# The diagonal products of a chunked SSD, issued in two halves of 64 stationary columns

## The chip, the core and the metric

The kernel runs on one NeuronCore of one Trainium2 chip. TensorE multiplies: a load instruction puts the stationary operand (up to 128 x 128) into its array, and a product instruction streams the moving operand (up to 512 columns) through it into PSUM. VectorE, ScalarE and GpSimd work elementwise; 16 DMA engines move data. The metric is the device time of one execution in microseconds (us), as the median of the runs on record. Matrix products are done in one of two number forms: plain fp32, or F32R, a rounded fp32 for which the kernel splits each operand into a high and a low part and sums three products (the helper `mm3`, lines 403 to 406).

## The reference, cut to what matters

One layer of an encoder over 512 tokens of width 1024: layer norm, a mixer of neighbourhood attention and a bidirectional Mamba-2 SSD, and a squared-ReLU MLP. The SSD has 8 groups of 4 heads of width 64, state 128, and works in 4 chunks of 128 tokens. The part that the change touches is the product within a chunk, `y_diag`:

```
seg = a_cs[..., :, None] - a_cs[..., None, :]
lmat = jnp.exp(jnp.where(tril, seg, -jnp.inf))
cb = jnp.einsum('bclgn,bcsgn->bcgls', cc, bc)
y_diag = jnp.einsum('bcgls,bcgrls,bcsgrp->bclgrp', cb, lmat, xc)
...
y = y_f + y_b + xs * d_skip
```

For each group, chunk and head that is a 128 x 128 matrix of decays times scores, applied to 128 x 64 values. The kernel joins both directions in one such matrix.

## The kernel before, in words

Five stages follow each other on TensorE: the first layer norm and its transposes, the projections with the SSD (L977 last at 470.7 us), attention, the merge of the branches with the output projection, and the MLP. In the first two, the work is a list of steps (`op(engine, us, function, reads, writes)`). A planner (`Plan`, from line 109) ranks them by the longest way to the end, with the hand-given price of each step, and orders each engine's steps; the order at the beginning is written out by hand (`HEAD`, line 72). Steps marked `filler` are the large projections: they fill TensorE whenever no SSD step is ready.

For each of the 8 groups, `ssd` (from line 849) does on TensorE: transposes of B and x to tokens (L858, L878), the scores `cb` = B C for each chunk (L868), the chunk states `st` (L929, L941), the diagonal products `yd` (L977), and the products with the states, `yo` (L991). The matrix for `yd` is made in the tile `bc`: a DMA brings the running sums of the decays, VectorE and GpSimd subtract (L963), VectorE joins the directions (L967), ScalarE takes the exponential (L969), VectorE multiplies by the scores (L971).

`f_yd` (lines 975 to 979) then issues, for one chunk, four products, one a head: stationary is `bc()[:, 1, h, :]`, 128 x 128, moving is `xtok`, 128 x 64. The results of four heads lie beside each other in 256 columns of the tile `yd`, a PSUM bank that holds two chunks. The pool of banks has one for `yd` (`BANKS`, line 41). Both operands are plain fp32; each call shows in the trace as two loads and two products. `f_yd` is one step of the plan with a price of 0.9 us, and is called 32 times. VectorE adds `yd` to the off-diagonal part (L1011), and GpSimd multiplies the sum by the gate (L1021); transposed and split, it is the moving operand of the projection `ps_sbr`.

Three other places of TensorE's work matter below. `ps_dt` (helper lines 404 to 406) uses F32R tiles of 64 stationary columns (`wh_dt`, `wl_dt`, L584 and L585), and writes partitions 0 to 63. `ps_acsT` (L739) has plain fp32 operands, 32 stationary columns, and writes partitions 0 to 31. `tp_dt` (L681) transposes tiles of 64 rows.

## Time and profile before

| | |
|---|---|
| median of 3 runs | 1184.75 us (1184.36 to 1185.21) |
| profiled execution | span 1182.6 us |
| TensorE, products | 1159.1 us busy, 6138 instructions |
| TensorE, loads of weights | 990.3 us busy, 6138 instructions |
| VectorE, ScalarE, GpSimd | 757.7, 614.7, 545.2 us busy |
| DMA | 149.19 MB, 126 GB/s |
| L977, products | 256, in 31.0 us, 270 ns each |
| L977, loads | 256, in 31.5 us, 191 ns each |

PE are TensorE's products, PEld its loads, which run beneath the products. A form such as `128*64 128x256` means 128 rows and 64 columns of the array in use, and a moving operand of 128 x 256. The start of a product in the trace is when the array's queue takes it: a product that has to wait for its weights is shown longer than one that does not. Ends of products are modelled.

### The profile page before, as it was taken

The numbers are of one execution on the slowest core, as the hardware profiler recorded it, in microseconds if no ns is written. First come the engines' busy times: TensorE is split into PE (matmuls) and PEld (weight loads), VectorE is DVE, ScalarE is ACT, GpSimd is POOL, SyncE is SP. The second block draws the span as 40 slices with busy tenths as digits, with TensorE's granted clock in tenths as the row PEclk, the third lists the DMA queues.
The fourth block names the chain that finished last, engine by engine and source line by source line (L and its number), as shares of the span: only waits on it lengthen the run. The fifth ranks groups of instructions, "written<-read, shape, count | busy, mean of one in ns | idle before, by whom it ended". The sixth has DMA issues, their size and how long they took to land.

```text
span 1182.6 us, 16453 instructions
## 1 busy us (share of the span) xinstructions
PE 1159.1 (98%) x6138; PEld 990.3 (84%) x6138; DVE 757.7 (64%) x1363; ACT 614.7 (52%) x1033; POOL 545.2 (46%) x588
## 2 busy tenths in 40 slices
PE   5999999999999999999999999999999999999997
PEld 5988798989888888888888888888988888878886
DVE  7757475666656656443789975556543658488856
ACT  6676573837354654423667864342253545365410
POOL 1268968777788786304567540016046121222000
PEclk9999999999999999999999999999999999999999
DMA  6353333333333331333333223544236977889511
GB/s 201 97 157 125 102 130 107 112 116 129 102 114 107 126 120 59 107 105 85 87 87 86 56 71 107 166 147 138 85 107 184 237 187 200 192 211 233 160 51 54
DMA packets 129407, 149.19 MB, mean 126 GB/s; under 512 B 22960, under 2 KB 101808, under 8 KB 129328
## 3 DMA queue, kind: packets, MB, share of 16 engines
q1 hardware_dynamic: 115696, 112.63, 31.0%
q0 software_dynamic: 13056, 34.61, 11.9%
q8 instruction: 48, 0.79, 0.3%
q10 hardware_dynamic: 576, 0.92, 0.2%
q14 instruction: 31, 0.25, 0.1%
HBM read 145.90 MB, written 2.23 MB: 125 GB/s over the span
## 4 chain that ended last, share of the span: by engine, by line
PE 86%; DMA 4%; DVE 4%; issue 2%; POOL 2%; ACT 1%; SPq 1%; DVEq 0%; POOLq 0%; ACTq 0%
PE ps_f L406 8%; PE ps_f L404 8%; PE ps_f L405 8%; PE ps_x L406 5%; PE ps_x L404 5%; PE ps_x L405 4%; PE ps_abr L1368 4%; PE ps_z L404 3%; PE ps_z L405 3%; PE ps_z L406 3%; PE ps_sbr L404 2%; PE ps_sbr L406 2%; PE ps_sbr L405 2%; PE yd L977 2%; DMA w2r<-in_w_ff 2%; PE ps_g L405 2%
## 5 line engine op out<-in xcount | busy, mean ns | idle before, releaser
L784 DVE SCALAR_TENSOR_TENSOR cv<-ps_x,pc,cv 128x511 f32<-128x511 f32 (+1 forms) x128 | 95.7, 748 | 25.6 <-ACT cv L776 22.0
L405 PE MATMUL ps_f<-h1Th,wl_f 128*128 128x512 f32 (+1 forms) x288 | 104.0, 365 | 0.0
L404 PE MATMUL ps_f<-h1Th,wh_f 128*128 128x512 f32 (+1 forms) x288 | 103.6, 365 | 0.0
L406 PE MATMUL ps_f<-h1Tl,wh_f 128*128 128x512 f32 (+1 forms) x288 | 102.0, 365 | 0.0
L1571 DVE TENSOR_TENSOR wl_f<-w2r,wh_f 128x1024 fp32r<-128x1024 f32 x42 | 50.0, 1220 | 62.5 <-ACT wh_f L1570 62.2
L404 PE MATMUL ps_z<-wh_z,hTh 128*128 128x256 f32 x256 | 75.2, 294 | 0.6 <-DVE cv L784 0.5
L406 PE MATMUL ps_z<-wl_z,hTh 128*128 128x256 f32 x256 | 71.5, 279 | 0.0
L405 PE MATMUL ps_z<-wh_z,hTl 128*128 128x256 f32 x256 | 71.5, 279 | 0.0
L1565 POOL DMA_DIRECT2D w2r<-in_w_ff x30 | 36.3, 1415 | 75.6 <-DMA w2r<-in_w_ff 49.0
L405 PE MATMUL ps_f<-wh_f,sql 128*128 128x512 f32 x168 | 65.3, 390 | 0.5 <-DVE sql L1571 0.5
L406 PE MATMUL ps_f<-wl_f,sqh 128*128 128x512 f32 x168 | 65.3, 390 | 0.1
L1570 ACT ACTIVATE wh_f<-w2r 128x1024 fp32r<-128x1024 f32 x42 | 42.6, 1052 | 43.1 <-DMA w2r<-in_w_ff 32.8
L404 PE MATMUL ps_f<-wh_f,sqh 128*128 128x512 f32 x168 | 64.9, 389 | 0.0
L1099 DVE TENSOR_TENSOR ysacc<-ps_sbr,ysacc 128x512 f32<-128x512 f32 x56 | 38.6, 690 | 39.9 <-PE ps_sbr L406 39.7
L404 PEld LDWEIGHTS ps_f<-h1Th,wh_f 128*128 128x128 f32 x288 | 53.9, 188 | 9.0 <-ACT rl L1672 0.2
L405 PEld LDWEIGHTS ps_f<-h1Th,wl_f 128*128 128x128 f32 x288 | 53.9, 188 | 8.7
L387 DVE TENSOR_TENSOR wl_f<-ws_f,wh_f 128x1024 fp32r<-128x1024 f32 x36 | 47.2, 1347 | 20.9 <-ACT wh_f L386 20.7
L406 PEld LDWEIGHTS ps_f<-h1Tl,wh_f 128*128 128x128 f32 x288 | 52.8, 188 | 8.7
L404 PE MATMUL ps_x<-hTh,wh_bc 128*128 128x512 f32 (+1 forms) x144 | 56.7, 394 | 0.0
L404 PE MATMUL ps_sbr<-yTh,wh_sbr 128*128 128x512 f32 x128 | 55.6, 434 | 0.7 <-ACT yTh L1076 0.4
L406 PE MATMUL ps_x<-hTl,wh_bc 128*128 128x512 f32 (+1 forms) x144 | 53.4, 371 | 1.7 <-DVE hTl L626 1.7
L404 PE MATMUL ps_x<-hTh,wh_x 128*128 128x512 f32 (+1 forms) x144 | 54.6, 379 | 0.0
(344 smaller groups left out, 3734.2 us busy)
## 6 DMA issues: line engine op xcount, KB each, us to landing
ws_f<-in_w_ff SPq DMA_DIRECT2D x20, 1024.0 KB
w2r<-in_w_ff POOLq DMA_DIRECT2D x18, 1024.0 KB, 7.6
bc<-acs_d SPq DMA_DIRECT2D x32, 512.0 KB
w2r<-in_w_ff POOLq DMA_DIRECT2D x30, 512.0 KB, 8.8
ws_bc<-in_w_in SPq DMA_DIRECT2D x16, 512.0 KB
ws_x<-in_w_in SPq DMA_DIRECT2D x8, 1024.0 KB
ws_z<-in_w_in SPq DMA_DIRECT2D x8, 1024.0 KB
ws_g<-in_w_in SPq DMA_DIRECT2D x8, 1024.0 KB
```

Source lines behind the costliest of these rows:

```text
L387: (eng[i] if isinstance(eng, tuple) else eng).tensor_tensor(out=lo[:, k], in0=st[:, k], in1=hi[:, k].bitcast(F32), op=ALU.subtract)
L404: nc.tensor.matmul(o, lh, rh, start=start, stop=False)
L405: nc.tensor.matmul(o, ll, rh, start=False, stop=False)
L406: return nc.tensor.matmul(o, lh, rl, start=False, stop=stop)
L784: op("DVE", 0.75, lambda j=j, o=o, n=n: nc.vector.scalar_tensor_tensor(out=acc()[:, o], in0=ps()[:, n], scalar=tap(j), in1=acc()[:, o], op ...
L977: nc.tensor.matmul(yd()[:, c % 2, h * HD : (h + 1) * HD], bc()[:, 1, h, :], xtok()[:, c, h * HD : (h + 1) * HD], start=True, stop=True)
L1099: op("DVE", 0.69, lambda d=d, ps=ps: nc.vector.tensor_tensor(out=ysacc[:, d, :], in0=ps(), in1=ysacc[:, d, :], op=ALU.add), r=[(ps.name, 0 ...
L1368: ins.append(nc.tensor.matmul(pss[j], u, v, start=k + p == 0, stop=k == KD - 1 and p == 2))
L1565: nc.gpsimd.dma_start(t, rows(i, n, c, k), accum_op=ALU.add)
L1570: nc.scalar.activation(hi[:, k], x, AF.Copy)
L1571: low = nc.vector.tensor_tensor(out=lo[:, k], in0=x, in1=hi[:, k].bitcast(F32), op=ALU.subtract)
```

## The change

In `f_yd` each product is issued as two: the first has the stationary columns 0 to 63 and writes partitions 0 to 63 of the bank, the second has columns 64 to 127 and writes partitions 64 to 127. The moving operand is the same for both. There are 256 calls in place of 128; the step of the plan, its price, its reads and writes, and the tiles stay as they are.

```diff
                 def f_yd(c=c, bc=bc, yd=yd):
                     for h in range(HPG):
-                        nc.tensor.matmul(yd()[:, c % 2, h * HD : (h + 1) * HD], bc()[:, 1, h, :],
-                                         xtok()[:, c, h * HD : (h + 1) * HD], start=True, stop=True)
+                        for rows in (slice(0, 64), slice(64, P)):
+                            nc.tensor.matmul(yd()[rows, c % 2, h * HD : (h + 1) * HD],
+                                             bc()[:, 1, h, rows],
+                                             xtok()[:, c, h * HD : (h + 1) * HD], start=True, stop=True)
                 op("PE", 0.9, f_yd, r=[(bc.name, 1), (xtok.name, c2)], w=[(yd.name, c % 2)])
```

## The prediction

> **What bounds the kernel now.** I read the page first, then the busy times by stage, the groups by line with shapes apart, and last the timeline of TensorE and of its weight loads around single instructions.

> ```profile
> span 1182.6 us, 16453 instructions
> PE 1159.1 (98%) x6138; PEld 990.3 (84%) x6138; DVE 757.7 (64%) x1363; ACT 614.7 (52%) x1033; POOL 545.2 (46%) x588
> PE   5999999999999999999999999999999999999997
> 78.00:471.00 393.00, 391.60 (x2246) 338.68 (x2245) 249.12 (x416) 225.61 (x337) 312.85 (x321) 1.00 0.35 112
> L977 PE MATMUL yd<-xtok,bc 128*128 128x64 f32 x256 | 31.0, 270 | 0.1
> L977 PEld LDWEIGHTS yd<-xtok,bc 128*128 128x128 f32 x256 | 31.5, 191 | 1.8 <-DVE bc L971 0.6 <-DVE yz L1011 0.2
> ```

> TensorE is busy in nearly all of every slice. All 256 products of L977 lie between 78 and 471 us (fourth line; its columns are the length of the stage, then the busy time of PE, PEld, DVE, ACT and POOL). There PE has 391.6 of 393.0 us, at the full granted clock (1.00), and VectorE only 249 and GpSimd 313. So 1.4 us are free in the stage, and a microsecond that L977 gains or loses on TensorE is a microsecond of the kernel. The executions on record have a median of 1184.75 us; the profiled one has a span of 1182.6, and I add changes to the one and the other alike (2.1 us apart).

> The 256 products are the 128 calls of the code (8 groups, 4 chunks, 4 heads): a call on plain fp32 operands shows as two loads and two products. What a pair costs is in one run of them on the engine's timeline:

> ```profile
> 104.93 0.39 PE L406 MATMUL ps_x<-hTl,wh_x 128*128 128x512 f32 x1
> 105.16 1.89 PE L977 MATMUL yd<-xtok,bc 128*128 128x64 f32 x16
> 106.86 0.48 PE L404 MATMUL ps_x<-hTh,wh_x 128*128 128x512 f32 x1
> 107.17 0.39 PE L405 MATMUL ps_x<-hTh,wl_x 128*128 128x512 f32 x1
> ```

> The columns are start, length, engine and line. The product after the run stands with 0.48 us where its kind takes 0.39; 0.09 of that is waiting for its weights, so it works from 106.95. From 105.16 to there are 1.79 us for 16 pairs: 0.112 us a pair.

> Is that the product or the load? Three widths of load are in the trace:

> ```profile
> L404 PEld LDWEIGHTS ps_dt<-hTh,wh_dt 128*64 128x64 f32 x16 | 2.3, 146 | 0.0
> L739 PEld LDWEIGHTS ps_acsT<-tri,dts 128*32 128x32 f32 x16 | 1.6, 109 | 0.5 <-DVE acsT L742 0.3
> 22.03 0.13 PEld L404 LDWEIGHTS ps_dt<-hTh,wh_dt 128*64 128x64 f32 x1
> ```

> 191 ns for 128 columns and 109 for 32: 82 ns for 96 columns, 0.854 ns a column, on a fixed latency that the stream hides. (64 columns should then show 136; the last row has 0.13, and the mean of 146 includes the slower first microseconds.) A load of 128 columns occupies 0.109 us, one of 64 columns 0.055, one of 32 columns 0.027. The product streams 64 moving columns; the 128 moving columns of ps_acsT (below) go at 1.06 us for eight, less the 0.27 of the last record, over seven steps: 0.11 each, so 64 take 0.055. **So L977 waits for its loads:** 0.109 us of loading hides 0.055 of multiplying, and 0.003 a pair is lost on top.

> **The change part by part.** *The products.* 128 calls become 256, each with half the columns. PE gets 256 loads and 256 products more (512 of each for L977), and a load of 64 columns now takes as long as the product that hides it, 0.055 us. With the same 0.003 on top I take 0.058 a pair. From below, 0.055 is what either side alone allows if the halves go one after the other; from above stands the shortest run of small products in the trace:

> ```profile
> 33.30 0.32 PEld L681 LDWEIGHTS tp_dt<-cst,dtT 64*128 64x128 f32 x4
> ```

> Four loads in 0.32 us, of which the last is 0.137: 0.061 a step. So halving the columns by itself buys next to nothing: two pairs at 0.058 stand for one at 0.112.

> *The edges of each run.* TensorE now works with 64 columns of its array in these products and with 128 in the neighbours. The nearest rows are of two kinds and disagree. The products of ps_acsT use 32 columns, and are plain fp32 with two loads a call, as L977 is:

> ```profile
> 58.95 0.28 PE L405 MATMUL ps_z<-wh_z,hTl 128*128 128x256 f32 x1
> 59.07 0.28 PE L406 MATMUL ps_z<-wl_z,hTh 128*128 128x256 f32 x1
> 59.27 1.06 PE L739 MATMUL ps_acsT<-tri,dts 128*32 128x128 f32 x8
> 59.27 0.79 PEld L739 LDWEIGHTS ps_acsT<-tri,dts 128*32 128x32 f32 x8
> 60.26 0.30 PEld L730 LDWEIGHTS pcs<-dts,tri 128*128 128x128 f32 x2 [0.20 <-issue]
> 61.34 1.06 PE L739 MATMUL ps_acsT<-tri,dts 128*32 128x128 f32 x8
> 62.33 0.50 PE L404 MATMUL ps_g<-hTh,wh_g 128*128 128x512 f32 x1
> 62.67 0.40 PE L405 MATMUL ps_g<-hTh,wl_g 128*128 128x512 f32 x1
> ```

> Going in: the last ps_z product starts at 59.07 and is through its 0.12 at 59.19; the next load starts only at 59.27, instead of beneath that product, so 0.09 us (unrounded) pass empty and then the load itself lies bare. Going out: the eighth product starts at 59.27 + 1.06 - 0.27 = 60.06 and is through at 60.17; the next load comes at 60.26, 0.09 later, with nothing that it waited for ("issue"). The second exit, at 62.33, is alike, and the product behind it shows 0.50 for a usual 0.39: 0.11 of bare load. The array runs empty, and the load that follows hides under nothing.

> The other rows are of ps_dt: 64 columns, but of the rounded type F32R (L584) and one load a call:

> ```profile
> 22.03 0.28 PE L406 MATMUL ps_x<-hTl,wh_bc 128*128 128x256 f32 x1
> 22.14 0.28 PE L404 MATMUL ps_dt<-hTh,wh_dt 128*64 128x256 f32 x1
> 22.25 0.28 PE L405 MATMUL ps_dt<-hTh,wl_dt 128*64 128x256 f32 x1
> 22.37 0.28 PE L406 MATMUL ps_dt<-hTl,wh_dt 128*64 128x256 f32 x1
> 22.48 0.28 PE L404 MATMUL ps_x<-hTh,wh_bc 128*128 128x256 f32 x1
> ```

> Here the step stays 0.11 in and out: no edge at all. So an edge costs between nothing and the ps_acsT figure. I take the latter: L977 has its number type and its two loads, and its lower halves must leave the array at partitions 64 to 127, which ps_dt, at partition 0, never asks for.

> [...]

> *The sum.* L977 stands in 22 unbroken runs on PE: 12 of 8 products and 10 of 16 (256 in all), the first and the last of them:

> ```profile
> 78.55 1.00 PE L977 MATMUL yd<-xtok,bc 128*128 128x64 f32 x8
> 469.04 1.89 PE L977 MATMUL yd<-xtok,bc 128*128 128x64 f32 x16
> ```

> Before, the runs cost 256 x 0.112 = 28.7 us, from the first product to the start of the next stranger, its load included. After, a run pays 0.09 + 0.055 going in, 0.058 for every step but the first, and 0.055 (last product) + 0.09 + 0.109 going out. That is 0.40 a run, 22 x 0.40 = 8.8 us, and (512 - 22) x 0.058 = 28.4 us of steps. 8.8 + 28.4 - 28.7 = **+8.5 us**. With 0.055 a step it is +7.1, with 0.061 +10.0, and if entering takes another 0.09 as well, +12.

> *What else moves.* VectorE's sums of yd wait for the last product:

> ```profile
> DVE yz L1011 <- PE yd L977: 9.9, 7, 2.6
> ```

> They get their data some 0.2 to 0.4 us later per run; VectorE has 144 us free in the stage, and TensorE does not stand on it: cost nothing, and at most these 0.4 us x 22 where a chain through yz, yT and ps_sbr should become the last one. The planner's price of the step (0.9 us) is not edited, so I take the order on PE as it is. No DMA, tile or wait is added but the instructions to be fetched: 512 more beside 16,453, on a queue that has 0.3% of the DMA time; I cost it at nothing. If the cover for that were gone, it would show as gaps of "issue" on PE.

> So: 1182.6 + 8.5 = 1191.1 us of span, and 1184.75 + 8.5 = 1193.3 us for the median.

> **The rivals.**

> *The halves run at the same time (faster).* The upper half uses columns 0 to 63 of the array and the lower half 64 to 127; if each has its own path for weights, the lower half's loads run under the upper half's products and loads. Two pairs then take the time of one, 0.029 a pair: 490 x 0.029 = 14.2, + 8.8 - 28.7 = -5.7 us, 1179.1. It decides for faster by 0.2% (2.4 us; that is also about what a measurement of this kernel tells from no change) where a step is below 0.036 us, since 22 x 0.40 + 490 x 0.036 - 28.7 = -2.3. Overlap by half (0.043) gives about +1. For it: nothing in the trace forbids it. Against it: within a run, today's loads come strictly one per product, and the order of issue is both passes of the upper half, then both of the lower, so that loads of one half stand in line behind a product that waits for the load before it. [...]

> *No edges (the division is not made, or costs nothing).* As at ps_dt. 512 x 0.058 = 29.7 us, and at the 22 exits the wide load sticks out by 0.054 us: 1.2. Together +2.2 us, 1187.0; with 0.055 a step +0.7, 1185.4. This is also the case in which the change doesn't do what it says.

> *An edge at every half (much slower).* If going from the upper to the lower half empties the array too, each half pays 0.09 + 0.055 + 0.058 + 0.055 = 0.258 us: 256 x 0.258 = 66.0, + 22 exits x 0.2 = 4.4, - 28.7 = +41.7 us, 1226.5. For it: the trace has no product at any partition but 0. Against it: ps_acsT's eight products follow each other without a gap once the array is divided.

> **How the numbers follow.** The forecast has 0.46, the overlap of halves 0.26 (0.20 of it full, 0.06 partial and within 2.4 us), no edges 0.14 (0.09 within 2.4 us, 0.05 beyond), an edge at every half 0.12, a chain through VectorE or something unseen 0.02. Faster by over 0.2%: 0.20. Within 0.2%: 0.06 + 0.09 = 0.15. Slower: 0.46 + 0.05 + 0.12 + 0.02 = 0.65. The range runs from the full overlap, 1178.5 with a little to spare, to the forecast's dear end, 1197.0; the edge at every half is left outside. The slower cases alone, without that one, lie between 1191 and 1197.

> **What would show it.** L977 should have 512 products and loads of 64 columns, with loads of about 136 ns. Right would be: the load after each run starts some 0.2 us after the start of the last product before it, as at 60.26; the first load of a run no longer lies under the product before; inside a run a step of 0.055 to 0.061 us; PE's work from 78 us on longer by 8 to 9 us, and every other stage as it was. Steps near 0.03 would prove the overlap, runs without gaps at their ends the second rival, a gap every two pairs the third. The forecast is wrong also if other engines' waits on PE change the order or the length of the stage by more than the runs of L977 do.

## The result, and the profile after

The changed kernel takes 1177.97 us in the median (1177.48 to 1179.06), the kernel before 1184.55. The ratio is 0.9943 with an interval of 0.9929 to 0.9957: 6.6 us faster, 5.1 to 8.4. The forecast was 8.5 us slower. The profiled execution is 6.4 us shorter than the one before.

The page of the changed kernel:

```profile
span 1176.2 us, 16965 instructions
PE 1153.0 (98%) x6394; PEld 977.1 (83%) x6394; DVE 765.4 (65%) x1363; ACT 614.9 (52%) x1033; POOL 545.5 (46%) x588
```

The groups by line of the changed kernel, with shapes apart, for L978 (the line of the product, L977 before); the columns are busy time, mean ns of one, and idle time before it:

```profile
L978 PE MATMUL yd<-xtok,bc 128*64 128x64 f32 x512 | 19.7, 226 | 0.2 <-DVE bc L971 0.2
L978 PEld LDWEIGHTS yd<-xtok,bc 128*64 128x64 f32 x512 | 16.7, 137 | 6.9 <-issue 3.1 <-DVE cbd L887 0.7 <-DVE yz L1013 0.7
```

The count has doubled to 512, the width is 64, and a load shows 137 ns, as foretold (136). But the time in which any of these products runs has fallen from 31.0 to 19.7 us, and 512 loads of 137 ns lie in 16.7 us: about four at any time, where one stream with the prediction's step of 0.058 us would have 137 / 58 = 2.4 by estimate, and the one-sided run below has 2.2 (512 loads of 138 ns in 31.5 us).

TensorE's timeline around a run of four heads and two chunks, and around one of a single chunk:

```profile
104.08 0.39 PE L405 MATMUL ps_x<-hTh,wl_x 128*128 128x512 f32 x1
104.31 0.39 PE L406 MATMUL ps_x<-hTl,wh_x 128*128 128x512 f32 x1
104.62 1.15 PE L978 MATMUL yd<-xtok,bc 128*64 128x64 f32 x32
105.71 0.50 PE L404 MATMUL ps_x<-hTh,wh_x 128*128 128x512 f32 x1
106.04 0.39 PE L405 MATMUL ps_x<-hTh,wl_x 128*128 128x512 f32 x1
...
138.89 0.39 PE L406 MATMUL ps_x<-hTl,wh_bc 128*128 128x512 f32 x1
139.20 0.69 PE L978 MATMUL yd<-xtok,bc 128*64 128x64 f32 x16
139.82 0.50 PE L404 MATMUL ps_x<-hTh,wh_bc 128*128 128x512 f32 x1
```

Read the long run first. 32 products start within 1.15 - 0.22 (the last record) = 0.93 us: a step of 0.030, about half of the 0.055 that one load occupies the array by the prediction's estimate. In the single records they come in twos: two products start 7 ns apart, and the next two 0.0583 us after them. Then the edges. The product before starts at 104.31 and streams for 0.23 (104.08 to 104.31), to 104.54; L978 starts at 104.62. The product behind has 0.50 for a usual 0.39, so it works from 105.82. From 104.54 to 105.82 the run costs 1.28 us; 32 x 0.029 of it are steps, and 0.35 is the price of the two edges. The short run costs 139.93 - 139.12 = 0.81, of which 0.34 is edges. Before, the long run cost 1.79. A short one:

```profile
140.04 0.39 PE L406 MATMUL ps_x<-hTl,wh_bc 128*128 128x512 f32 x1
140.27 1.00 PE L977 MATMUL yd<-xtok,bc 128*128 128x64 f32 x8
141.08 0.48 PE L404 MATMUL ps_x<-hTh,wh_bc 128*128 128x512 f32 x1
```

141.17 - 140.27 = 0.90. So 12 short runs save 0.09 each and 10 long ones 0.51: 6.2 us, where the span is 6.4 shorter. The order of all other instructions on TensorE, VectorE, ScalarE and GpSimd is the same in both traces. Outside the runs there are differences of both signs that nearly cancel. The product before the first run starts 0.35 us earlier (77.97 for 78.32), before anything of the change has run. Between the first run and the last, TensorE loses 0.7 us net: a wait of 0.5 for `cv` at ps_z is gone, one of 0.4 for `cv` has come at L858, and the rest was not followed. Behind the last run some 0.6 us are gained, most of it a wait in the MLP. In the groups by line before, and in those after:

```profile
L405 PE MATMUL ps_f<-wh_f,sql 128*128 128x512 f32 x168 | 65.3, 390 | 0.5 <-DVE sql L1571 0.5
```

```profile
L405 PE MATMUL ps_f<-wh_f,sql 128*128 128x512 f32 x168 | 65.3, 390 | 0.0
```

That wait of 0.5 us comes and goes between the kernels tried here; nothing in the change touches it.

### The profile page after: what moved, and what is told of

Same layout as the page of the kernel before. It is cut to its first block, busy times and chain, and to the rows that moved or that the text cites. A ratio compares the mean times of both kernels' runs of the same rounds, so it can differ in the third digit from the quotient of the medians.

```text
span 1176.2 us, 16965 instructions
## 1 busy us (share of the span) xinstructions
PE 1153.0 (98%) x6394; PEld 977.1 (83%) x6394; DVE 765.4 (65%) x1363; ACT 614.9 (52%) x1033; POOL 545.5 (46%) x588
## 2 busy tenths in 40 slices
PE   5999999999999999999999999999999999999997
## 4 chain that ended last, share of the span: by engine, by line
PE 84%; DVE 5%; DMA 5%; issue 2%; ACT 2%; POOL 1%; SPq 1%; DVEq 0%; POOLq 0%; ACTq 0%
PE ps_f L404 8%; PE ps_f L406 8%; PE ps_f L405 8%; PE ps_x L404 4%; PE ps_x L406 4%; PE ps_x L405 4%; PE ps_abr L1370 4%; PE ps_z L404 3%; PE ps_z L405 3%; PE ps_z L406 3%; PE ps_sbr L404 2%; PE ps_sbr L406 2%; PE ps_sbr L405 2%; DMA w2r<-in_w_ff 2%; PE ps_g L405 2%; PE ps_g L404 2%
## 5 line engine op out<-in xcount | busy, mean ns | idle before, releaser
L405 PE MATMUL ps_f<-h1Th,wl_f 128*128 128x512 f32 (+1 forms) x288 | 104.1, 365 | 0.0
L404 PE MATMUL ps_f<-h1Th,wh_f 128*128 128x512 f32 (+1 forms) x288 | 103.6, 365 | 0.0
L406 PE MATMUL ps_f<-h1Tl,wh_f 128*128 128x512 f32 (+1 forms) x288 | 102.0, 365 | 0.0
L404 PE MATMUL ps_z<-wh_z,hTh 128*128 128x256 f32 x256 | 75.2, 294 | 0.0
L406 PE MATMUL ps_z<-wl_z,hTh 128*128 128x256 f32 x256 | 71.5, 279 | 0.0
L405 PE MATMUL ps_z<-wh_z,hTl 128*128 128x256 f32 x256 | 71.5, 279 | 0.0
L405 PE MATMUL ps_f<-wh_f,sql 128*128 128x512 f32 x168 | 65.3, 390 | 0.0
L406 PE MATMUL ps_f<-wl_f,sqh 128*128 128x512 f32 x168 | 65.2, 390 | 0.1
L404 PE MATMUL ps_f<-wh_f,sqh 128*128 128x512 f32 x168 | 64.9, 389 | 0.0
L404 PEld LDWEIGHTS ps_f<-h1Th,wh_f 128*128 128x128 f32 x288 | 53.9, 188 | 8.9
L405 PEld LDWEIGHTS ps_f<-h1Th,wl_f 128*128 128x128 f32 x288 | 53.9, 188 | 8.7
L406 PEld LDWEIGHTS ps_f<-h1Tl,wh_f 128*128 128x128 f32 x288 | 52.8, 188 | 8.7
L404 PE MATMUL ps_x<-hTh,wh_bc 128*128 128x512 f32 (+1 forms) x144 | 56.6, 393 | 0.0
L404 PE MATMUL ps_sbr<-yTh,wh_sbr 128*128 128x512 f32 x128 | 55.8, 436 | 0.8 <-ACT yTh L1078 0.4
L406 PE MATMUL ps_x<-hTl,wh_bc 128*128 128x512 f32 (+1 forms) x144 | 53.5, 371 | 1.8 <-DVE hTl L626 1.8
L404 PE MATMUL ps_x<-hTh,wh_x 128*128 128x512 f32 (+1 forms) x144 | 54.6, 379 | 0.0
```

The lines of the kernel that those rows point to most:

```text
L404: nc.tensor.matmul(o, lh, rh, start=start, stop=False)
L405: nc.tensor.matmul(o, ll, rh, start=False, stop=False)
L406: return nc.tensor.matmul(o, lh, rl, start=False, stop=stop)
```

## The experiments

The theory after the result, an inference from the step of 0.030 us and the gaps above: the halves lie in different columns of the array and run side by side, each at the pace of one stream (0.058 us a pair), and every run pays 0.35 us for its edges. The trace does not name the columns of a load. Rivals: the narrow loads and products are quicker in themselves; the edges are not a price of the run. All times are medians beside runs of the kernel before on the same chip.

| kernel | us | before there | ratio (interval) |
|---|---|---|---|
| changed | 1177.97 | 1184.55 | 0.9943 (0.9929 to 0.9957) |
| both halves on one side | 1198.76 | 1184.73 | 1.0122 (1.0108 to 1.0137) |
| changed, sum split | 1185.77 | 1183.66 | 1.0014 (1.0005 to 1.0023) |
| blocks of four heads | 1184.34 | 1184.73 | 0.9997 (0.9988 to 1.0006) |
| blocks of two heads | 1179.85 | 1183.66 | 0.9967 (0.9955 to 0.9978) |
| quarters | 1177.34 | 1184.73 | 0.9939 (0.9926 to 0.9952) |
| one step for both chunks | 1191.23 | 1184.73 | 1.0064 (1.0047 to 1.0081) |
| first chunk moved down | 1183.73 | 1183.66 | 0.9998 (0.9989 to 1.0008) |
| the same, quarters | 1182.53 | 1183.66 | 0.9992 (0.9981 to 1.0002) |
| second chunk moved up | 1177.74 | 1184.09 | 0.9948 (0.9936 to 0.9960) |
| the same, quarters | 1177.15 | 1184.09 | 0.9942 (0.9930 to 0.9954) |

**Both halves on one side.** The same loads and products, but all of them write partitions 0 to 63; by the theory no two are then in different columns. The lower half of the result is left out, so VectorE's sum becomes a sum and a copy.

```diff
-                            nc.tensor.matmul(yd()[rows, c % 2, h * HD : (h + 1) * HD],
+                            nc.tensor.matmul(yd()[:64, c % 2, h * HD : (h + 1) * HD],
...
-                    out=y()[:, c, :], in0=yd()[:, c % 2], in1=t2()[:, c % 2], op=ALU.add),
+                    nc.vector.tensor_tensor(out=y()[:64, c, :], in0=yd()[:64, c % 2],
+                                            in1=t2()[:64, c % 2], op=ALU.add)
+                    nc.vector.tensor_copy(y()[64:, c, :], t2()[64:, c % 2])
```

> Both halves are written to partitions 0 to 63 (the lower half of the result is left out, and the sum takes only the off-diagonal part there, with one more small VectorE instruction). Same number of loads and products, same widths, same edges, but no two in different halves of the array. Side by side (my theory): the step in a run goes back from 0.029 to about 0.058 us, the runs cost 22 x 0.35 + 512 x 0.058 = 37.4 us against 28.9 before the change, and the time is 8.5 us over the kernel before, about 1193. Rival, the narrow loads and products are quicker in themselves (a step of 0.029 without any overlap): about 1178, as the changed kernel.

Its group of products:

```profile
L978 PE MATMUL yd<-xtok,bc 128*64 128x64 f32 x512 | 34.5, 224 | 0.8 <-DVE yz L1014 0.5 <-PE ps_x L406 0.4
```

A long run on its TensorE timeline:

```profile
186.34 0.39 PE L406 MATMUL ps_sbr<-yTl,wh_sbr 128*128 128x512 f32 x1
186.66 2.08 PE L978 MATMUL yd<-xtok,bc 128*64 128x64 f32 x32
188.67 0.50 PE L404 MATMUL ps_sbr<-yTh,wh_sbr 128*128 128x512 f32 x1
```

32 products start within 2.08 - 0.22 = 1.86 us, 0.060 a step with the bare first load in it; the records inside the run are 0.0585 apart. The run costs 188.78 - 186.57 = 2.21 us, 0.93 more than with both sides, and the 512 products fill 34.5 us for 19.7. So narrow products are not quicker in themselves: two of them cost 0.117 us on one side, one of 128 columns before 0.112. Nor is the cause that both halves write the same addresses here: in the kernel with blocks of four heads below, products of one side that go to new addresses with each head start 0.058 us apart too, as long as they are alone (the first five loads of a run lie in 0.37 us). The edges are as they were (0.09 before the run, 0.11 of waiting behind it), though here nothing leaves the array but at partitions 0 to 63. The time, however, is 14.0 us over the kernel before, not 8.5; the next run asks why.

**Changed, sum split.** VectorE's edit alone.

> The changed kernel with VectorE's sum as in the one-sided run: the lower half of the product is left out of the sum, which becomes two instructions. It tells how much of that run's 14 us is VectorE's edit. The runs of L978 there account for 9.3 us over the kernel before, so 4 to 5 us should be VectorE's: 1182 to 1183. Rival, VectorE is covered: 1178, and the rest of the 14 us belongs to the serial halves.

1185.77: the edit costs about 8 us (7.8 by the medians, 8.4 by the ratios), more than expected. The group of the new instruction:

```profile
L1016 DVE COPY yz<-t 64x256 f32<-64x256 f32 x32 | 25.8, 807 | 0.6
```

The 32 copies of 64 x 256 take 807 ns in the mean, where the sum of 128 x 256 took 417. The mean mixes two cases: in this trace 13 copies meet no work of GpSimd (one of them 9 ns of it) and take 291 to 293 ns each; the other 19 run while GpSimd works and take 313 to 2462 ns (the longest with GpSimd busy for 2312 of them). The 25.8 us of copies became some 8 us of the kernel. Against this kernel the one-sided run is 13 us slower (13.0 and 12.8): that is what writing both sides is worth over writing one. TensorE's own account (34.5 - 19.7 = 14.8 us) is a little more.

**Blocks of four heads, and of two.** The same instructions; the upper halves of four (or two) heads first, then their lower halves.

```diff
-                    for h in range(HPG):
-                        for rows in (slice(0, 64), slice(64, P)):
+                    for rows in (slice(0, 64), slice(64, P)):
+                        for h in range(HPG):
```

> The four upper halves of a chunk first, then its four lower halves; the instructions are the same. If only a neighbour in the queue can run beside the one ahead (a look-ahead of a few instructions), most of the overlap is lost: a step of 0.058 but for one place a chunk, about 1192. If the queue looks 16 instructions ahead or more, the lower halves start while the upper ones run, and the time stays at 1178.

Neither: 1184.34, no gain left. A long run on its TensorE timeline:

```profile
181.76 0.39 PE L406 MATMUL ps_sbr<-yTl,wh_sbr 128*128 128x512 f32 x1
182.08 1.54 PE L978 MATMUL yd<-xtok,bc 128*64 128x64 f32 x32
183.55 0.50 PE L404 MATMUL ps_sbr<-yTh,wh_sbr 128*128 128x512 f32 x1
```

The first loads of another run, on the timeline of loads cut off at 105.426:

```profile
105.14 0.37 PEld L978 LDWEIGHTS yd<-xtok,bc 128*64 128x64 f32 x5 [0.35 <-DVE cbd L887]
```

> Blocks of two heads: the upper halves of two heads, their lower halves, then the next two heads. In the run with blocks of four heads a block's first load starts beside the sixth load of the block ahead, with five instructions of it still to go. If that is the reach of the look-ahead, a block of four pairs is joined by the next one from its second load on, and the step stays at 0.029 us but for about 0.1 us at the ends of each run: 22 x 0.1 = 2 us over the changed kernel, 1180. Rival, blocks lose in proportion to their length (the loss of 6.4 us halved): 1181 to 1182, with a step of about 0.033. Rival, nothing but a direct neighbour runs beside: 1190.

1179.85: 1.9 us over the changed kernel by the medians, 2.8 by the ratios. The theory had 2, its nearest rival 3 to 4, so the time alone does not part these two. The run:

```profile
180.76 0.39 PE L406 MATMUL ps_sbr<-yTl,wh_sbr 128*128 128x512 f32 x1
181.08 1.20 PE L978 MATMUL yd<-xtok,bc 128*64 128x64 f32 x32
182.21 0.50 PE L404 MATMUL ps_sbr<-yTh,wh_sbr 128*128 128x512 f32 x1
```

182.32 - 180.99 = 1.33 us, 0.05 over the changed kernel's 1.28; half of what blocks of four lose would be 0.20. In the records the lower side stands still once a run, for 0.05 us. That speaks for the theory. But the number is an inference from these two kernels, and not exact: at the start of each run here the lower side's first load starts 13 ns after the upper side's, with six instructions of the upper block still to start (three loads and three products). Five or six, then; blocks of other lengths were not tried.

**Quarters.** `for rows in (slice(q, q + 32) for q in range(0, P, 32))`.

> Four products of 32 columns in place of two of 64. Side by side: loads of 32 columns take 0.027 us, but the product still streams 64 columns in 0.055 us, so a call still takes two steps of about 0.058 and the edges stay; the time stays at 1178 within 1 us. Rival, the load is still what a step waits for: a call falls from 0.117 to about 0.06 and the time by up to 7 us, to 1171. Rival, the issue of the instructions (8 in 0.058 us) becomes the limit: slower, by 7 us if a step doubles.

1177.34, within the uncertainty of the changed kernel's time. A run, with 64 products of 32 columns:

```profile
103.84 0.39 PE L406 MATMUL ps_x<-hTl,wh_x 128*128 128x512 f32 x1
104.16 1.10 PE L978 MATMUL yd<-xtok,bc 128*32 128x64 f32 x64
105.19 0.50 PE L404 MATMUL ps_x<-hTh,wh_x 128*128 128x512 f32 x1
```

105.30 - 104.07 = 1.23 us, 0.05 less than with halves. 64 products start within 1.10 - 0.22 = 0.88 us, one every 0.014; in the records four of them come every 0.0557 us, where with halves two come every 0.0583. By the theory these are four streams beside each other. By the estimates of the prediction (0.027 for a load of 32 columns, 0.055 for the product) each now waits for its product. So halves would already stand where load and product are about equal, with little left in narrower loads (0.6 us by the medians); twice the instructions show no cost.

**Fewer edges.** One step of the plan for both chunks of a bank:

> The products of both chunks of a bank as one step of the plan, so that there are 16 runs in place of 22. If each run pays its two edges (0.35 us), 6 runs fewer save 2.1 us: about 1176, if the new order of the plan costs nothing elsewhere. Rival, the edges are no cost of a run: 1178. The order of the other work changes too, which can cost or save some us beside.

1191.23, 6.5 us slower than the kernel before. The plan came out in another order; besides, the move written by hand (`MOVE`, line 106) then puts one multiplication by the scores ahead of its exponential, for chunk 3 of the first group, so that the matrix of this chunk is no longer the one meant. With so much moved, the time says nothing on edges. The two next keep the order and move four steps:

```diff
+        for i, j in pairs.values():
+            a, b = order.index(i), order.index(j)
+            if 0 < sum(self.ops[k]["e"] == "PE" for k in order[a + 1 : b]) < 5:
+                order.remove(i)
+                order.insert(order.index(j), i)
```

> Order of the changed kernel, but in four groups the first chunk's products are issued after the few products for the chunk states that stood between the two chunks: 18 runs in place of 22, nothing else moved on TensorE. If each run pays its edges of 0.35 us: 4 x 0.35 = 1.4 us less, 1176.6. Rival, the edges are a cost of the instructions and not of a run, or the delay of the first chunk is paid elsewhere: 1178.

> Quarters of 32 columns and 18 runs together: 0.6 us from the quarters (a step of 0.0557 in place of 0.0583, waiting for the product and no more for the load) and 1.4 us from the edges: 1176.0. Rival, either gain is noise: 1177 to 1178.

18 runs, and yet 1183.73 and 1182.53. SyncE's timeline of the changed kernel, then of the moved one:

```profile
232.81 2.01 SPq L959 DMA_DIRECT2D bc<-acs_d  x2
```

```profile
234.36 0.89 SPq L968 DMA_DIRECT2D bc<-acs_d  x2
```

The group of the moved kernel whose wait on PE grew:

```profile
L413 PE MATMUL ps_sbr<-yTh,wh_sbr 128*128 128x512 f32 x128 | 56.0, 438 | 4.2 <-DVE ysacc L1110 3.5 <-ACT yTh L1087 0.4
```

The same group in the changed kernel:

```profile
L404 PE MATMUL ps_sbr<-yTh,wh_sbr 128*128 128x512 f32 x128 | 55.8, 436 | 0.8 <-ACT yTh L1078 0.4
```

The products of the first chunk read a `bc` tile. Run some 1.6 us later, they release it later; the DMA that refills it is issued at 234.36 instead of 232.81; VectorE's subtraction, next in its queue, waits for the data, the sum `ysacc` behind it is late, and TensorE waits for the bank that `ysacc` frees: 4.2 us before ps_sbr, for 0.8 in the changed kernel. That is 3.4 of about 6 us lost. TensorE also waits 0.5 us at the chunk states for GpSimd's `xw` and 0.3 at ps_z for `cv`, which it does not in the changed kernel; the rest was not followed. Moving the second chunk up instead avoids the late DMA:

```diff
-                order.remove(i)
-                order.insert(order.index(j), i)
+                order.remove(j)
+                order.insert(order.index(i) + 1, j)
```

> As the moved kernel, but the second chunk's products go up to the first's, and the four products for the chunk states behind both: 18 runs again, and the decay tiles of the first chunk are released as early as in the changed kernel. The moved kernel issued the DMA into them 1.55 us later, and VectorE and TensorE waited behind it. If that wait, and not the edges, made it slower, this one shows the edges alone: 4 x 0.35 = 1.4 us less than the changed kernel, 1176.6. Rival, merging runs does not pay however it is done (the products find their input late, or the chunk states are): 1178 or over.

> The same with quarters of 32 columns: 0.6 us less again, 1176.0. Rival: 1177 to 1178.

1177.74 and 1177.15: the moved kernel's loss is gone, but the expected 1.4 us do not show. At the first of the four places, on the timeline of loads of the kernel with halves:

```profile
235.11 0.41 PEld L950 LDWEIGHTS st<-xw,btok 128*128 128x128 f32 x2
235.87 0.30 PEld L950 LDWEIGHTS st<-xw,btok 128*128 128x128 f32 x2 [0.35 <-POOL xw L922]
```

TensorE comes to the next chunk states earlier, and its loads wait 0.35 us there for GpSimd's `xw`. By the starts of the products behind it, 0.15 us of the 0.35 are kept at the first place and at the second, and nothing at the other two; besides, a wait of 0.3 us for `cv` at ps_z is back. None of the quarters or moves is faster than the changed kernel beyond the uncertainty.

## Why the prediction was wrong

**What bounds.** Right: L977 stood on the path with its full length (its runs save 6.2 us, the span 6.4), and waited for its loads: with the same 64 moving columns a pair takes 0.0585 us in the one-sided run, where a load has 64 columns, and took 0.112 with 128. A load of 64 columns shows 137 ns (136 foretold) for 191, and one stream of them has the step that was taken, 0.058.

**The step that failed** is the first of "The change part by part": "So halving the columns by itself buys next to nothing: two pairs at 0.058 stand for one at 0.112." It counts the halves one after the other. In the trace a pair comes every 0.029 us, side by side by the theory: 490 x 0.029 = 14.2 us of steps where the sum had 28.4. This was the first rival, whose 1179.1 is 1.1 us from the measured time; it had a chance of 0.26 (0.20 for the full overlap), and its reason against was that the loads of one half stand behind a waiting product of the other half. The runs show otherwise: in the changed kernel a second load starts 7 ns after the first of a run, in blocks of two heads the first load of the lower block 13 ns after that of the upper, with six instructions of the upper still to start, and in blocks of four it came only beside the sixth, with five. By the inference above the other side is held up only when some five or six instructions wait. The reason was drawn from the strict alternation of loads and products before the change, where all of them use all columns; a row in which two column ranges are in use at once was not in the trace, and the weight was put on what it showed of one.

**The edges.** Right in place and nearly in size: 0.35 us a run, 22 times, 7.7 us. The sum counts the first step of a run into the edge; counted so, it is 1.28 - 31 x 0.029 = 0.38 for the sum's 0.40. So the two rows of the trace that disagreed were rightly weighed: L978 behaves as ps_acsT, not as ps_dt. Of the two reasons given, the partitions are not needed, since the one-sided run has the same edges at partitions 0 to 63. Whether the number type is the cause was not tried. The edges are why a halving of 28.7 us brings 6 and not 14: 12 of the 22 runs have one chunk, and save 0.09 us.

**The other rivals.** No edges: refuted by the gaps. An edge at every half: refuted by the step.

**What else moves.** Nearly right for this change: the order stayed, and one wait of 0.4 us came (L858) where others went. But the ground given, that VectorE has 144 us free, is no ground: the split sum gave it 25.8 us of copies, and about 8 came out at the end; and a delay of some 1.6 us in the refilling of a few tiles left TensorE waiting 3.4 us more.

**The range** was 1178.5 to 1197.0. It ended at the full overlap's 1179.1 with 0.6 to spare. The runs saved 6.2 us where that rival had 5.7, which gives 1178.6, just inside. The 0.6 us from there to 1177.97 have no single cause: the kernel before came out 0.2 lower beside the changed one (1184.55 for 1184.75), the span shrank by 0.2 more outside the runs, and the changed kernel's own times spread from 1177.48 to 1179.06.

## What to carry to other kernels

Here products of 64 moving columns waited for their loads (0.112 us a pair), and two with half the stationary columns each, written to partitions 0 to 63 and 64 to 127, went at a step of 0.030 us, for 0.060 with both on one side. Where products wait like that, try it, with the two directly behind each other (6.6 us gained) and not in blocks (with blocks of four heads nothing was), and count a price per unbroken run, here 0.35 us, so that long runs gain (0.51 of 1.79 us) and short ones hardly do (0.09 of 0.90). Before a step is moved to lengthen a run, look at which tiles it releases and which DMA waits for them: here that cost 3.4 us, to save edges of 1.4. An engine with free time over a stage can still be late at the one place where another waits: here VectorE had 144 us free, and 25.8 us of copies cost about 8.

## What the runs showed of the hardware that was not expected

- Loads of the lower halves started ahead of instructions of the upper halves that were issued before them: with blocks of four heads the first load of the lower block started 2 ns after the sixth of the upper one, with five instructions still waiting; at the start of a run with blocks of two heads it came 13 ns after the first, with six.
- 64 products of 32 columns took 1.10 us, one start every 0.014 us; 32 of 64 columns took 1.15, one every 0.030.
- A VectorE copy of 64 x 256 took 291 to 293 ns when GpSimd did no work meanwhile, and up to 2462 when it did (L1016 of the kernel with the sum split). The sum of 64 x 256 from PSUM, just before it (L1014), took 397 to 417 ns in both cases. In the changed kernel the same shows at L1296 (`sc<-sc,sums`, 128 x 256): 28 of its instructions meet no work of GpSimd and take 341 to 355 ns, the other 36 take 352 to 1452; the sum from PSUM (L1013) takes 403 to 426 throughout.
